# Moving gate tiles of a projection from attention's filling to the stage of the masks

## The chip, the cores and the metric

One core of a Trainium2 chip runs the whole kernel. The metric is device time in microseconds, the median of several runs. Its engines are TensorE (PE, with its weight loads as PEld), VectorE (DVE), ScalarE (ACT), GpSimd (POOL) and SyncE (SP), which issues the loads.

## The reference, cut to what matters

Two layers over 1088 tokens (1024 of a prompt, 64 of a sample) and 1024 features. The change lies in layer 0, where one input projection feeds a sparse attention (a) and a short convolution (b), each with a gate of its own:

```python
q, k, v, ga, qi, ki, wi, gb, gc, xin, gz = _split(h @ w_in, EVEN_SPLITS)
...
top_val, top_idx = lax.top_k(score, topk)
...
logits = jnp.einsum('bqgrd,bqkgd->bqgrk', q, kg).astype(jnp.float32) * (HEAD_DIM ** -0.5)
p = jax.nn.softmax(logits, axis=-1).astype(v.dtype)
...
a_out = o * jax.nn.silu(ga)
...
b_out = gb * y * jax.nn.silu(gz)
out = jnp.concatenate([a_out, b_out], axis=-1) @ w_out
```

Eight heads attend in four pairs; a query's keys are its 256 best by the indexer's score (144 for the sample).

## The kernel before, in words

A projection tile is 128 output features. It takes 72 matmuls: three chunks of tokens (364, 364, 360), eight feature tiles each, and three products each, since weights and activations are split into a high and a low part (`w_hi`, `w_lo`, `ah`, `al`). A weight tile passes through SP (load of `w_raw`), ACT (`w_hi`, L238) and POOL (`w_lo`, L239); there are two places for it, used in turn, so that a tile's `w_hi` can be written only when PE is through with the tile before the last.

Layer 0 goes in stages. The indexer's scores come first, then the search for the threshold of every row (`topk`), beside which PE runs most of the projections. Then DVE makes the masks (`mask`, L592 to L607, seven blocks of rows, tile `bias`). Attention follows (`attend`, L711): for each of the four head pairs t, eight blocks of 128 queries and one block of the sample. For a block PE makes logits (L620), DVE adds the mask and finds the extreme (L622), ACT takes the exponential (L625), POOL scales (L627), PE transposes (L650), ACT and DVE split the result into high and low part (L276 `pth`, L277 `ptl`), and PE multiplies by the values (L658). At a pair's start ACT and POOL prepare its queries (`qst`, L698 and L699).

Eleven projection tiles are left for this time: three of q, four of gate b (`GB`), four of gate a (`GA`), in a fixed order (L47):

```python
ATTN_TILES = [(Q_, 1), (Q_, 2), (Q_, 3), (GB, 0), (GB, 1), (GA, 0), (GB, 2), (GA, 1), (GB, 3), (GA, 2), (GA, 3)]
```

They are a generator, `tiles()` in `layer0` (L919), that issues one matmul (L262) for each call of `next`. Gate a of pair t multiplies the finished output of that pair, so it is held back:

```python
kind, t = left[0]
while kind == GA and self.done <= t:
    yield
```

`BEFORE` calls are made ahead of attention (L932); they come into the program behind the masks, but PE has no other work then and runs them early. `RATE` holds three counts for each pair: calls after each piece of logits (L621), after each pass of `weighted` (L660), and after its transposes (L652). A call that meets a held tile issues nothing. What is left after attention runs behind it. A chunk of gate b is read out of PSUM by DVE (L894, tile `bo`), of gate a by ACT (L909, tile `ga`), which takes the SiLU when the tile is whole (L911); POOL then multiplies (L912). After the last tile ACT and DVE split the mixer's output into `ah` and `al`, and the output projection (`op`, L247) begins. A scheduler decides in what order the instructions stand in each engine's queue.

Of the kernel before, what the change touches and what calls it, by code (L numbers as in the profile page):

```python
# [84 lines left out]
ORDER = [(0, 1, 2, 3, 4, 5, 6, 7)] + [(7, 0, 6, 1, 5, 2, 4, 3)] * 3  # L85


BEFORE = 255
RATE = ((1, 1, 3),) * 4


def cut(n):
# [5 lines left out]
class Trunk:  # L98
# [663 lines left out]
    def layer0(self):  # L762
# [41 lines left out]
        with ExitStack() as es:  # L804
# [74 lines left out]
            with self.pool("attn", "right") as ap:  # L879
# [39 lines left out]
                def tiles():  # L919
                    while left:  # L920
# [3 lines that stand above are left out]
                        key, w = ahead.pop(0)  # L924
                        assert key == (kind, t)
                        fetch()
                        yield from self.steps(w, evacs[kind](t), n=1)
                        left.pop(0)
                        yield

                self.side = tiles()
                for _ in range(BEFORE):  # L932
                    next(self.side)
                for t in range(4):
                    while (Q_, t) in left:
                        next(self.side)
                    self.rate = RATE[t]
                    st = self.pair_stack(ap, t)
# [282 lines left out]
```

## Time and profile before

| | us |
|---|---|
| median of 3 runs (1161.16 to 1162.71) | 1161.26 |
| the profiled execution | 1162.17 |
| its span, first to last instruction | 1160.5 |
| PE busy | 1087.5 (94%) |
| DVE busy | 670.2 (58%) |
| ACT busy | 519.3 (45%) |
| POOL busy | 440.1 (38%) |

The span is what the trace covers; the profiled execution's own time is 1.7 us longer. Busy times are sums over the whole span, and the stages differ: a change in one is read from the rows of that stage, which a later section has.

### The profile page before, as it was taken

What the parts mean: (1) busy time and instruction counts of PE and PEld (TensorE: products, weight loads), DVE (VectorE), ACT (ScalarE), POOL (GpSimd) and SP (SyncE); (2) the same over time, 40 slices, a digit from 0 to 9 for tenths busy, and PEclk for the clock granted to TensorE, in tenths of its full rate; (3) what the DMA queues carried; (4) which work ended last, traced back from release to release, by engine and by line L of the source; (5) the groups of instructions that cost most, each with busy time, mean ns of one, the idle gap of its engine ahead of it and who ended that gap; (6) DMA issues with size and microseconds to landing.
All of it is one profiled execution on the core that took longest, in us unless ns stands there. A gap on an engine that the chain in (4) does not pass through costs nothing.

```text
span 1160.5 us, 18892 instructions
## 1 busy us (share of the span) xinstructions
PE 1087.5 (94%) x7255; PEld 1044.7 (90%) x7255; DVE 670.2 (58%) x1657; ACT 519.3 (45%) x976; POOL 440.1 (38%) x454
## 2 busy tenths in 40 slices
PE   5899999999999449999999899999999999999997
PEld 4789689999999439989899899999999999999996
DVE  4711799998886987767675524521186055247134
ACT  5232586856777246777666313521121211135111
POOL 2634223466548225464431326531143111154222
PEclk9999999999999769999999999999999999999999
DMA  9745511211101000000002410111112111131012
GB/s 361 302 155 191 201 29 55 80 52 38 37 19 54 25 14 19 19 19 20 19 20 82 160 59 31 44 55 37 37 47 91 37 37 36 38 108 38 1 65 91
DMA packets 26074, 81.84 MB, mean 71 GB/s; under 512 B 3072, under 2 KB 9984, under 8 KB 23552
## 3 DMA queue, kind: packets, MB, share of 16 engines
q1 hardware_dynamic: 25984, 80.63, 19.7%
q8 instruction: 57, 0.93, 0.3%
q14 instruction: 33, 0.27, 0.1%
HBM read 74.50 MB, written 6.12 MB: 69 GB/s over the span
## 4 chain that ended last, share of the span: by engine, by line
PE 81%; DVE 7%; ACT 5%; POOL 3%; issue 3%; DMA 1%; SPq 0%; POOLq 0%; DVEq 0%; ACTq 0%
PE pj L247 40%; PE op L247 15%; PE pj L262 9%; PE av L658 3%; PE logit_ps L620 2%; PE p_ps L650 2%; PE ada_ps L153 2%; PE sgu_ps L1036 1%; PE score_ps L427 1%; PE first L318 1%; POOL w_lo L239 1%; POOL hf L329 1%; DVE cum L604 1%; PE score_ps L428 1%; DVE al L277 1%
## 5 line engine op out<-in xcount | busy, mean ns | idle before, releaser
L247 PE MATMUL pj<-ah,w_hi 128*128 128x364 f32 (+1 forms) x984 | 326.0, 331 | 1.0 <-ACT w_hi L238 1.0
L247 PE MATMUL pj<-al,w_hi 128*128 128x364 f32 (+1 forms) x984 | 323.8, 329 | 0.0
L247 PE MATMUL pj<-ah,w_lo 128*128 128x364 f32 (+1 forms) x984 | 323.1, 329 | 0.0
L239 POOL TENSOR_TENSOR w_lo<-w_raw,w_hi 128x1024 fp32r<-128x1024 f32 x63 | 158.0, 2510 | 341.3 <-ACT w_hi L238 336.4
L247 PEld LDWEIGHTS pj<-ah,w_hi 128*128 128x128 f32 x984 | 185.0, 188 | 2.0 <-ACT w_hi L238 1.3
L247 PEld LDWEIGHTS pj<-ah,w_lo 128*128 128x128 f32 x984 | 184.8, 188 | 0.3 <-issue 0.2
L247 PEld LDWEIGHTS pj<-al,w_hi 128*128 128x128 f32 x984 | 185.0, 188 | 0.0
L247 PE MATMUL op<-ah,w_lo 128*128 128x448 f32 (+2 forms) x384 | 126.2, 330 | 3.1 <-POOL w_lo L239 3.1
L247 PE MATMUL op<-al,w_hi 128*128 128x448 f32 (+2 forms) x384 | 126.5, 330 | 0.7 <-DVE al L277 0.6
L247 PE MATMUL op<-ah,w_hi 128*128 128x448 f32 (+2 forms) x384 | 126.9, 330 | 0.0
L238 ACT ACTIVATE w_hi<-w_raw 128x1024 fp32r<-128x1024 f32 x69 | 72.9, 1058 | 111.6 <-PE pj L247 83.2
L528 DVE TENSOR_SCALAR_CACHE_REDUCE cum<-S,cand 128x512 bf16<-128x512 f32 (+5 forms) x142 | 119.0, 838 | 2.0
L262 PE MATMUL pj<-ah,w_hi 128*128 128x364 f32 (+1 forms) x288 | 96.0, 334 | 0.0
L262 PE MATMUL pj<-ah,w_lo 128*128 128x364 f32 (+1 forms) x288 | 95.2, 330 | 0.0
L262 PE MATMUL pj<-al,w_hi 128*128 128x364 f32 (+1 forms) x288 | 95.1, 330 | 0.0
L976 DVE SCALAR_TENSOR_TENSOR x<-op,mod,x 128x192 f32<-128x192 f32 (+2 forms) x64 | 30.5, 497 | 108.2 <-PE op L247 108.2
L555 ACT ACTIVATE junk<-S,cand 128x896 bf16<-128x896 f32 (+2 forms) x78 | 77.7, 996 | 24.4 <-DVE m L558 20.6
L627 POOL TENSOR_SCALAR S<-S,sm 128x384 f32<-128x384 f32 (+8 forms) x68 | 50.8, 753 | 87.1 <-DVE sm L626 72.7
L620 PE MATMUL logit_ps<-kp,qst 128*128 128x384 f32 (+5 forms) x192 | 49.6, 366 | 33.2 <-DVE sm L622 32.6
L247 PEld LDWEIGHTS op<-ah,w_lo 128*128 128x128 f32 x384 | 73.1, 190 | 5.4 <-POOL w_lo L239 3.5
L247 PEld LDWEIGHTS op<-al,w_hi 128*128 128x128 f32 x384 | 73.0, 190 | 3.4 <-DVE al L277 1.4
L247 PEld LDWEIGHTS op<-ah,w_hi 128*128 128x128 f32 x384 | 73.0, 190 | 2.0
(242 smaller groups left out, 1973.9 us busy)
## 6 DMA issues: line engine op xcount, KB each, us to landing
w_raw<-in_w SPq DMA_DIRECT2D x53, 512.0 KB, 3.4
ada<-in_ada_w SPq DMA_DIRECT2D x19, 1024.0 KB, 7.8
w_raw<-in_wo SPq DMA_DIRECT2D x16, 512.0 KB, 3.4
x<-in_x SPq DMA_DIRECT2D x8, 544.0 KB, 6.5
bo<-in_ada_w SPq DMA_DIRECT2D x4, 1024.0 KB, 6.9
x<-in_x SPq DMA_DIRECT2D x1, 1792.0 KB, 10.2
out_y<-x SPq DMA_DIRECT2D x1, 1792.0 KB, 6.6
x<-in_x SPq DMA_DIRECT2D x1, 1536.0 KB, 8.2
```

What stands on the lines that cost most here:

```text
L153: nc.tensor.matmul(pt[32 * g:32 * g + 32, 0:P], self.cs[:, kt, :], raw(kt)[:, g * P:(g + 1) * P], start=kt == 0, stop=kt == KT - 1, tile_p ...
L238: nc.scalar.activation(hi, raw, AF.Copy)
L239: (nc.gpsimd if lo_eng == "pool" else nc.vector).tensor_sub(lo, raw, hi)
L247: last = self.nc.tensor.matmul(ps, wt[:, kt, :], at[:, kt, c0:c1], start=n == 0, stop=n == len(mms) - 1)
L262: self.nc.tensor.matmul(ps, wt[:, kt, :], at[:, kt, a:b], start=kt == 0 and i == 0, stop=kt == KT - 1 and i == 2)
L528: V.tensor_scalar(junks[0][:, 0:SW[j]], self.S[:, span(j)], thr, 0.0, op0=OP.is_lt, op1=OP.add, accum_out=col(cv, j))
L555: nc.scalar.activation(junks[1][:, 0:SW[j]], self.S[:, span(j)], AF.Sign, scale=-1.0, bias=col(cand, j), accum_out=col(cv, j))
L620: mm = nc.tensor.matmul(pt[:, 0:w], lhs, keys[i][:, g, s], start=i == 0, stop=i == 1)
L627: nc.gpsimd.tensor_scalar(p, p, st[:, 3:4], 0.0, op0=OP.mult, op1=OP.add)
L650: mm = nc.tensor.transpose(pt[0:r, o:o + P], p[:, j * P:j * P + r], self.ident)
L658: mm = nc.tensor.matmul(av[:, 0:m], self.vs[0:r, vbase + j, g, :], t[0:r, o:o + m], start=j == 0 and i == 0, stop=j == nj - 1 and i == 1)
L976: nc.vector.scalar_tensor_tensor(x[:, t, a:b], ps[:, a:b], self.mod[l][:, 16 + t, j:j + 1], x[:, t, a:b], op0=OP.mult, op1=OP.add)
```

## The change

Two numbers change. `BEFORE` goes from 255 to 435 calls, and the count after the transposes goes from 3 to 1 for every pair. The order of the tiles stays.

```diff
-BEFORE = 255
-RATE = ((1, 1, 3),) * 4
+BEFORE = 435
+RATE = ((1, 1, 1),) * 4
```

Three places show what this does in the queues. The first is PE at the start of attention, where block 4 of pair 0 (two pieces of 320 keys) gets its logits while the first blocks are transposed. Before:

```order
L650 MATMUL p_ps_4262<-ident_69,S_603 128x128
L262 MATMUL pj_4217<-ah_64,w_lo_4104 128x364
L262 MATMUL pj_4217<-ah_64,w_hi_4103 128x364
L262 MATMUL pj_4217<-al_65,w_hi_4103 128x364
L650 MATMUL p_ps_4298<-ident_69,S_603 128x128
L620 MATMUL logit_ps_4438<-kp0_1903,qst_4233 128x320
L620 MATMUL logit_ps_4438<-kp1_1904,qst_4233 128x320
L650 MATMUL p_ps_4298<-ident_69,S_603 128x128 x3
L262 MATMUL pj_4307<-ah_64,w_hi_4103 128x360
L262 MATMUL pj_4307<-al_65,w_hi_4103 128x360
L620 MATMUL logit_ps_4454<-kp0_1903,qst_4234 128x320
L620 MATMUL logit_ps_4454<-kp1_1904,qst_4234 128x320
```

The same place now:

```order
L620 MATMUL logit_ps_4518<-kp0_1903,qst_4353 128x320
L620 MATMUL logit_ps_4518<-kp1_1904,qst_4353 128x320
L650 MATMUL p_ps_4380<-ident_69,S_603 128x128 x2
L620 MATMUL logit_ps_4522<-kp0_1903,qst_4353 128x320
L650 MATMUL p_ps_4410<-ident_69,S_603 128x128
L620 MATMUL logit_ps_4522<-kp1_1904,qst_4353 128x320
L650 MATMUL p_ps_4410<-ident_69,S_603 128x128 x3
L620 MATMUL logit_ps_4530<-kp0_1903,qst_4354 128x320
L620 MATMUL logit_ps_4530<-kp1_1904,qst_4354 128x320
L620 MATMUL logit_ps_4534<-kp0_1903,qst_4354 128x320
L620 MATMUL logit_ps_4534<-kp1_1904,qst_4354 128x320
```

The filling (L262, `pj`) is gone here, and up to the end of pair 0's sample block hardly any of it is left.

The second place is DVE while it makes the masks:

```order
 L604 SCALAR_TENSOR_TENSOR cum<-ones,cv,bias 128x384
+L894 TENSOR_TENSOR bo<-bo,pj 128x364
 L605 SCALAR_TENSOR_TENSOR bias<-cum,bias 128x384
 L606 SCALAR_TENSOR_TENSOR bias<-S,T,bias 128x384
 L604 SCALAR_TENSOR_TENSOR cum<-ones,cv,bias 128x512
 L607 TENSOR_SCALAR bias<-bias 128x384
+L894 TENSOR_TENSOR bo<-bo,pj 128x360
 L605 SCALAR_TENSOR_TENSOR bias<-cum,bias 128x512
 L606 SCALAR_TENSOR_TENSOR bias<-S,T,bias 128x512
```

Reads of gate b's PSUM now stand between the steps of the masks: these two and three more further on. Before, only one stood there.

The third place is ACT, and behind it POOL, just ahead of attention, where pair 0's queries are prepared. ACT:

```order
 L238 ACTIVATE w_hi<-w_raw 128x1024
 L772 ACTIVATE q<-pj 128x360
+L238 ACTIVATE w_hi<-w_raw 128x1024 x2
 L698 ACTIVATE qst<-q 64x512 x2
 L698 ACTIVATE qst<-q 64x576 x2
```

POOL:

```order
 L760 TENSOR_TENSOR bo<-bo,gc 128x64
 L584 MEMSET cv 128x1 x4
-L239 TENSOR_TENSOR w_lo<-w_raw,w_hi 128x1024 x2
+L239 TENSOR_TENSOR w_lo<-w_raw,w_hi 128x1024 x4
 L699 TENSOR_TENSOR qst<-q,qst 64x512 x2
 L699 TENSOR_TENSOR qst<-q,qst 64x576 x2
```

Two more weight tiles, of gate a 0 and gate b 2, are now split ahead of the queries.

## Rows read from the trace of the kernel before

**Rows 1.** Windows by stage: busy us of each engine (instructions), PEclk, DMA share, GB/s.
```profile
346.80:390.50 43.70, 43.65 (x265) 43.44 (x263) 34.41 (x116) 31.31 (x58) 29.82 (x33) 1.00 0.16 52
390.50:420.00 29.50, 0.00 (x0) 0.00 (x0) 29.19 (x34) 0.14 (x1) 1.95 (x2) 0.56 0.00 0
420.00:478.30 58.30, 54.83 (x349) 50.68 (x349) 43.70 (x149) 42.26 (x96) 30.32 (x35) 0.93 0.06 17
478.30:621.60 143.30, 138.48 (x950) 131.10 (x949) 98.17 (x305) 98.06 (x205) 58.68 (x58) 1.00 0.06 19
621.60:640.10 18.50, 18.42 (x102) 17.25 (x102) 12.96 (x28) 16.04 (x34) 7.07 (x3) 1.00 0.36 128
640.10:643.20 3.10, 0.04 (x1) 0.04 (x1) 2.86 (x4) 1.01 (x2) 3.01 (x1) 0.99 0.00 0
```

**Rows 2.** Chain of waits, in order of time (start, us, what).
```profile
347.01 34.43 PE pj L262 x207
...
476.94 1.45 PE av L658 x10
```

**Rows 3.** Timeline of PE around the masks (start, us, instruction, [idle before, releaser]).
```profile
390.05 0.40 PE L620 MATMUL logit_ps<-kp,qst 128*128 128x256 f32 x2
420.35 0.80 PE L620 MATMUL logit_ps<-kp,qst 128*128 128x256 f32 x2 [29.91 <-DVE sm L622]
```

**Rows 4.** Timeline of DVE in the masks and at their end.
```profile
392.86 0.52 DVE L894 TENSOR_TENSOR bo<-bo,pj 128x364 f32<-128x364 f32 x1
393.31 1.34 DVE L603 TENSOR_SCALAR bias<-S,T 128x896 bf16<-128x896 f32 x2
...
420.01 0.28 DVE L622 CUSTOM_DVE_ANT_0 S<-logit_ps,corner 128x128 f32<-128x128 f32 x1
```

**Rows 5.** Timeline of ACT, then POOL, ahead of attention; last, POOL near 638 us.
```profile
382.86 1.06 ACT L238 ACTIVATE w_hi<-w_raw 128x1024 fp32r<-128x1024 f32 x1 [1.44 <-issue]
...
384.18 2.69 ACT L698 ACTIVATE qst<-q 64x512 fp32r<-64x512 f32 x4
419.86 0.69 ACT L709 ACTIVATE kc<-kp 128x64 fp32r<-128x64 f32 x4 [32.99 <-DVE bias L606]
...
384.00 2.40 POOL L239 TENSOR_TENSOR w_lo<-w_raw,w_hi 128x1024 fp32r<-128x1024 f32 x1 [9.54 <-ACT w_hi L238]
386.48 6.04 POOL L699 TENSOR_TENSOR qst<-q,qst 64x512 fp32r<-64x512 f32 x4
...
637.98 5.13 POOL L239 TENSOR_TENSOR w_lo<-w_raw,w_hi 128x1024 fp32r<-128x1024 f32 x1 [9.08 <-ACT w_hi L238]
```

**Rows 6.** Windows at the start of attention, columns as in rows 1.
```profile
420.00:424.00 4.00, 1.68 (x4) 1.00 (x4) 1.16 (x9) 3.13 (x10) 1.23 (x3) 0.50 0.13 33
...
424.00:437.00 13.00, 12.96 (x75) 12.09 (x75) 11.86 (x49) 10.67 (x28) 7.98 (x13) 0.84 0.08 21
```

**Rows 7.** DVE's groups by line, 420 to 478.3 us: reads of gate b.
```profile
L894 DVE TENSOR_TENSOR bo<-bo,pj 128x364 f32<-128x364 f32 (+1 forms) x5 | 2.6, 526 | 0.8 <-PE pj L262 0.7
```

**Rows 8.** PE's waits, 478.3 to 621.6 us (total us, times, longest).
```profile
PE av L658 <- ACT pth L276: 1.2, 1, 1.2
PE p_ps L650 <- DVE ptl L277: 1.0, 1, 1.0
```

**Rows 9.** ACT's groups by shape in attention: queries, and the SiLU of gate a.
```profile
L698 ACT ACTIVATE qst<-q 64x576 fp32r<-64x576 f32 x6 | 4.0, 668 | 0.0
...
L911 ACT ACT_TABLE_LOAD x2 | 2.6, 1283 | 0.0
L911 ACT ACTIVATE ga<-ga 128x1088 f32<-128x1088 f32 x2 | 2.2, 1112 | 0.0
```

**Rows 10.** Windows of one us where PE's clock falls and rises, columns as in rows 1.
```profile
393.00:394.00 1.00, 0.00 (x0) 0.00 (x0) 1.00 (x3) 0.00 (x0) 0.00 (x0) 0.98 0.00 0
394.00:395.00 1.00, 0.00 (x0) 0.00 (x0) 1.00 (x3) 0.00 (x0) 0.00 (x0) 0.50 0.00 0
427.00:428.00 1.00, 1.00 (x6) 0.96 (x6) 0.97 (x4) 1.00 (x4) 0.62 (x2) 0.50 0.00 0
428.00:429.00 1.00, 1.00 (x9) 0.97 (x8) 0.48 (x4) 0.90 (x3) 1.00 (x2) 0.95 0.00 0
```

## The prediction

> **What bounds the kernel now.** I read the windows by stage first. In the masks PE does nothing for 29.5 us and DVE is busy for 29.19 of them [rows 1]: DVE sets that stage alone. PE stands at a pair of logits that needs DVE, with 29.91 us of idle before it [rows 3]. In attention PE is busy for 54.83 of 58.3 us up to the end of pair 0's sample block (its last multiplication by the values is in [rows 2]) and for 138.48 of 143.3 in the other three pairs, while DVE (43.70 and 98.17) and ACT (42.26 and 98.06) have room [rows 1]: PE is the bound, because the filling fills what the chain of a block leaves open. Then PE is dense until 640.1, and 3.1 us follow in which POOL makes a weight part that PE needs.
>
> One filling matmul costs 0.166 us: 207 of them take 34.43 us on the chain [rows 2].
>
> **What moves.** Counted in PE's queue, the filling is now 255 matmuls ahead of attention, 112 up to the end of pair 0's sample block, 349 in the rest of attention, 76 behind it. With the change it is 360, 5, 246 and 181. The words "three tiles" promise more than happens: of the 180 added calls only 105 issue a matmul (what was left of gate b 0, and gate b 1). The next tile is gate a 0, which is held until pair 0 is done, so 75 calls find nothing, and so do pair 0's own. Pair 0 loses its filling altogether, the others about 34 matmuls each, and 105 more run behind attention. PE's total work is the same; what decides is where it waits.
>
> **The masks.** 105 matmuls at 0.166 are 17.4 us, which lie inside PE's 29.5 idle us. On DVE, which sets this stage, five more reads of gate b come in. One holds DVE up by 0.45 us (392.86 to 393.31) [rows 4], so +2.3 us. Were DVE to wait for PE there it would cost more, but PE ends a chunk each 4 us and has the last one at 389.3 + 17.4 = 406.8, while the read of it stands behind the steps of the block of 896, which DVE reached after 409. I take 2.3; ends 2.3 and 4.
>
> **Pair 0.** Without filling DVE becomes the bound. It is busy for 43.70 us up to the end of the sample block [rows 1]; 2.6 of them are the five reads that move [rows 7], which leaves 41.1. The first 4 us hold 1.2 of it, since exponentials must come first [rows 6]; that start stays. The other 39.9 go at the share that DVE reaches when it is pressed. No row has attention without filling. The nearest is 424 to 437, where the first blocks run with few filling matmuls between them: 11.86 of 13 us, 0.91 [rows 6]. That gives 43.8 + 4 = 47.8 us in place of 58.3: -10.5. PE without its 112 matmuls (18.6 us) needs less than 40. For the ends I take shares of 0.95 (46.0 us, -12.3) and 0.88 (49.3 us, -9.0); the far end is the share in the other pairs, 98.17 of 143.3 or 0.69, at which nothing would be gained.
>
> **Pairs 1 to 3.** 103 matmuls fewer are -17.1 us if every one of them shortens the stretch. PE's waits there are short and come where ACT is held by something else: 1.2 us for `pth`, 1.0 for `ptl` [rows 8]. Such holds are the SiLU of gate a (table load 1.28, 1.11 for the tile, and the table of the exponential again) and the queries (four of 0.65) [rows 9], about 3 us each and two to a pair. In that time the chain moves on by some two passes, and each pass now has about two matmuls of filling instead of four, 0.33 us less cover: two holds of two passes are 1.3 us, say 1.5 a pair, 4.5 in all. So -12.6; ends -17.1 (no new waits) and -8.1 (3 us a pair).
>
> The trace shows PE busy for 0.97 of this stretch and its weight loads for 0.91 [rows 1]. The Trainium skill (Perfetto Trace Analysis, section Identifying the Most-Contended Engine) says that matmul busy time is a poor measure of TensorE's headroom and that the busy share of weight loads is a better one. By it 0.09 of the stretch is already loose and the removed matmuls would shorten it by 0.91 of 17.1 instead: an estimate of 1.5 us less gain, which would leave the sum at -1.9.
>
> **Behind attention.** 105 more matmuls at 0.166: +17.4. PE is busy for 18.42 of the 18.5 us there [rows 1], so nothing hides them. The three added tiles bring their weight splits to engines that have room. The 3.1 us behind it follow the last tile as before and stay.
>
> **The sum.** 2.3 - 10.5 - 12.6 + 17.4 = -3.4 us. The profiled execution took 1162.17, so 1158.8; the median of the runs lies 0.9 below it, so 1157.9 against 1161.26. With the ends of this case (-6.7 to +1.1) that is 1154.6 to 1162.4. A measurement of this kernel can tell about 0.2%, 2.3 us, from no change.
>
> **Rivals.**
>
> *The filling was cover, and waits take its place (slower).* In pair 0 each pass goes from PE's transposes over ACT's and DVE's split back to PE, with two buffers, and ACT has nearly as much to do as DVE (42.26 against 43.70) [rows 1]. If the two wait for each other, DVE's share is 0.80: 49.9 + 4 = 53.9 us, only -4.4; and the other pairs wait 3 us each. 2.3 - 4.4 - 8.1 + 17.4 = +7.2, that is 1168.5. It decides once pair 0 takes over 51.2 us, a DVE share under 0.845, with the other pairs as forecast. For it speaks that the share is 0.69 in the other pairs; against it, that PE and not the chain set their pace, and the 0.91.
>
> *All of it comes out (faster).* If pairs 1 to 3 have no new waits: 2.3 - 10.5 - 17.1 + 17.4 = -7.9, 1153.4. PE's few waits there [rows 8] speak for it; that each came with full filling around it speaks against it.
>
> *The first logits are late.* On ACT, pair 0's queries now stand behind the weights of gate a 0 and gate b 2, and the latter's place is free only when gate b 1 is through, at 406.8; they ran at 384.18 before [rows 5]. An ACT row that waits holds all behind it: `kc` waited 32.99 us and nothing else ran on ACT in them [rows 5]. From 406.8: `w_hi` 1.1, `w_lo` 2.4, two of POOL's four query parts 3.0 [rows 5]: 413.3, and DVE wants the logits at 420.0 + 2.3 = 422.3. Even with POOL at the 5.13 us that a `w_lo` took near 638 [rows 5], a factor of 2.1, it is 406.8 + 1.1 + 5.1 + 6.4 = 419.4. So it costs nothing; if all four parts are needed at the slow pace (425.8), 3.5 us, which makes the whole +0.1 and 1161.4. The Trainium skill (PSUM — Partial Sum Buffer, section Engine vs sequencer instructions) states that the queues of ScalarE, VectorE and GpSimd are strictly first in, first out. By that rule the queries cannot pass the waiting weights, and the trace agrees with its 32.99 us.
>
> *PE's clock stays low longer.* It fell to the 1.2 GHz level at 394 after 3.5 idle us and rose to 2.4 GHz at 428, when PE had been at work again since 423 [rows 10]. With the change it falls later, and pair 0 has nothing dense to raise it. PE's own work of pair 0 is at most 54.83 - 18.6 = 36.2 us in 47.8, so 10 us of it need 7.6 at the high level and 15.1 at the low one: 5.1 us lost for every 10 that it lasts longer, +1.7 in all and 1163.0. Against it: there was little filling before 428 either.
>
> **How the numbers follow.** The forecast 0.47, waits in the filling's place 0.28, all of it out 0.15, late logits 0.05, low clock 0.05. Faster by over 0.2%: some 0.7 of the forecast's range and all of the third, 0.48. Slower: most of the second and a little of the others, 0.26. Within 0.2%: 0.26. The range goes from a little under "all of it out" to the waits' 1168.5: 1152.5 to 1168.5. The likeliest case's own range is 1154.6 to 1162.4.
>
> **What would show it.** Right: PE idle between gate b 1 and the first DVE-bound logits about 13 to 16 us instead of 29.9; `bias` done 2 to 3 us later against the start of the masks; pair 0's stretch near 48 us with DVE over 0.88 busy; the other three near 131 us; 17 us more of dense filling behind attention. Wrong: pair 0 over 51 us with PE waiting for `pth` or `ptl` again and again; DVE waiting at L894 for PE in the masks; logits waiting for `qst`; a low clock beyond 435.

## The result and the profile after

The change makes the kernel slower: 1171.47 us (median of four, 1169.26 to 1173.27) against 1161.21, a ratio of 1.0084 with a 95% interval of 1.0063 to 1.0105. The profiled execution took 1170.45 us with a span of 1168.7, 8.2 more than before. It came to the masks 2.2 us sooner than the execution of before (first L602 at 379.24 against 381.44), in a part that the change does not touch, so the stages have to explain 10.4.

The windows by stage of the changed kernel, cut at the same events as those of every kernel below: the first step of the masks (L602), the first logits that DVE reads (L622), the last multiplication by the values of each pair's sample block (L658), and the first matmul of the output projection. Columns as in rows 1.

```profile
379.20:424.20 45.00, 27.43 (x160) 26.65 (x158) 44.78 (x55) 6.28 (x11) 17.28 (x7) 0.83 0.11 38
424.20:475.20 51.00, 43.70 (x245) 34.91 (x246) 40.51 (x144) 40.00 (x94) 26.91 (x33) 0.90 0.03 9
475.20:520.70 45.50, 43.33 (x276) 38.91 (x275) 34.56 (x109) 30.80 (x69) 17.46 (x20) 0.94 0.00 1
520.70:567.50 46.80, 43.21 (x281) 37.79 (x281) 35.31 (x117) 35.94 (x76) 23.36 (x24) 1.00 0.04 12
567.50:611.90 44.40, 42.88 (x292) 39.77 (x292) 26.31 (x79) 23.15 (x51) 9.07 (x10) 1.00 0.04 13
611.90:642.90 31.00, 30.38 (x182) 30.08 (x182) 8.14 (x17) 15.62 (x28) 12.20 (x5) 1.00 0.32 110
```

The kernel before, cut in the same way: the masks, the three later pairs, and the part behind attention (pair 0 is in [rows 1]).

```profile
381.40:420.00 38.60, 9.05 (x57) 8.84 (x55) 38.25 (x50) 4.10 (x8) 8.22 (x5) 0.66 0.05 17
...
478.40:526.60 48.20, 45.73 (x311) 42.60 (x311) 34.67 (x109) 36.46 (x75) 23.45 (x23) 1.00 0.07 23
526.60:575.50 48.90, 47.72 (x327) 45.13 (x327) 35.84 (x116) 34.53 (x76) 22.42 (x24) 1.00 0.04 12
575.50:621.60 46.10, 44.94 (x313) 43.28 (x313) 27.67 (x80) 26.96 (x55) 12.71 (x13) 1.00 0.07 24
621.60:634.20 12.60, 12.60 (x76) 12.60 (x77) 7.06 (x13) 10.55 (x21) 4.94 (x2) 1.00 0.51 184
```

| stage | before | changed | difference | forecast |
|---|---|---|---|---|
| masks | 38.6 | 45.0 | +6.4 | +2.3 |
| pair 0 | 58.4 | 51.0 | -7.4 | -10.5 |
| pairs 1 to 3 | 143.2 | 136.7 | -6.5 | -12.6 |
| behind attention, up to the output projection | 12.6 | 31.0 | +18.4 | +17.4 |
| from the output projection on | 526.3 | 525.8 | -0.5 | 0 |
| sum | | | +10.4 | -3.4 |

All four signs are as forecast, and the work moved as the queues said: PE issues 160 matmuls in the masks where there were 57, and 182 behind attention where there were 76. What is wrong is the size of three of the four terms.

**In the masks** DVE is busy throughout (44.78 of 45 us) and does not wait for PE at the reads of gate b. But some of its steps take longer. Timeline of DVE, changed kernel:

```profile
385.60 1.80 DVE L603 TENSOR_SCALAR bias<-S,T 128x384 bf16<-128x384 f32 x4
...
394.43 2.77 DVE L606 SCALAR_TENSOR_TENSOR bias<-S,T,bias 128x512 bf16<-128x512 f32 x1
...
406.92 2.43 DVE L607 TENSOR_SCALAR bias<-bias 128x768 bf16<-128x768 bf16 x1
409.27 2.15 DVE L605 SCALAR_TENSOR_TENSOR bias<-cum,bias 128x896 bf16<-128x896 bf16 x1
...
413.42 3.48 DVE L604 TENSOR_TENSOR_SCAN cum<-ones,cv,bias 128x1024 bf16<-128x1024 f32 x1
```

The same steps before:

```profile
387.80 5.14 DVE L603 TENSOR_SCALAR bias<-S,T 128x384 bf16<-128x384 f32 x4
...
399.23 0.75 DVE L606 SCALAR_TENSOR_TENSOR bias<-S,T,bias 128x512 bf16<-128x512 f32 x1
...
409.06 0.33 DVE L607 TENSOR_SCALAR bias<-bias 128x768 bf16<-128x768 bf16 x1
409.31 1.08 DVE L605 SCALAR_TENSOR_TENSOR bias<-cum,bias 128x896 bf16<-128x896 bf16 x1
...
411.50 2.34 DVE L604 TENSOR_TENSOR_SCAN cum<-ones,cv,bias 128x1024 bf16<-128x1024 f32 x1
```

And POOL in the changed kernel:

```profile
393.79 2.86 POOL L239 TENSOR_TENSOR w_lo<-w_raw,w_hi 128x1024 fp32r<-128x1024 f32 x1 [9.57 <-ACT w_hi L238]
405.77 3.36 POOL L239 TENSOR_TENSOR w_lo<-w_raw,w_hi 128x1024 fp32r<-128x1024 f32 x1 [9.13 <-ACT w_hi L238]
409.22 8.88 POOL L699 TENSOR_TENSOR qst<-q,qst 64x512 fp32r<-64x512 f32 x4
```

A DVE step that is long is one that ran beside POOL: L606 at 394.43 beside the first weight split, L607 at 406.92 beside the second, L605 and L604 beside the queries. Before, the queries stood beside L603 (6.04 us from 386.48 [rows 5]), and there L603 took 5.14 us in place of 1.80. So this cost was in the kernel already, 3.3 us of it; the change moved it and made it larger.

**In attention** PE now waits in many small pieces. Waits of PE's weight loads in pairs 1 to 3 of the changed kernel (475.2 to 611.9; total us, times, longest):

```profile
PEld av L658 <- ACT pth L276: 4.2, 7, 1.1
PEld av L658 <- DVE ptl L277: 3.5, 8, 0.5
...
PEld p_ps L650 <- DVE ptl L277: 0.7, 2, 0.4
```

The same waits before (478.4 to 621.6):

```profile
PEld p_ps L650 <- DVE ptl L277: 1.4, 2, 1.3
PEld av L658 <- ACT pth L276: 1.4, 1, 1.4
...
PEld av L658 <- DVE ptl L277: 0.6, 2, 0.3
```

Together they are 8.4 us where they were 3.4. The matmuls' own idle time, of which [rows 8] has the two longest pieces before, grew by less: 7.3 us in place of 4.8, by the windows above.

The clock fell a second time, at the end of pair 0. A line of PE's timeline in the changed kernel, then windows of one us, columns as in rows 1:

```profile
473.21 0.30 PE L658 MATMUL av<-pth,vs 128*128 128x128 f32 x1 [1.40 <-DVE q L722]
```

```profile
472.00:473.00 1.00, 0.00 (x0) 0.00 (x0) 0.67 (x3) 0.69 (x3) 1.00 (x3) 1.00 0.00 0
473.00:474.00 1.00, 0.79 (x7) 0.82 (x7) 0.34 (x2) 0.00 (x0) 0.37 (x1) 0.91 0.00 0
474.00:475.00 1.00, 1.00 (x5) 0.88 (x4) 0.00 (x0) 0.59 (x1) 0.00 (x0) 0.50 0.00 0
...
480.00:481.00 1.00, 1.00 (x7) 0.97 (x7) 0.68 (x2) 0.29 (x1) 0.90 (x1) 0.68 0.00 0
```

PE did nothing in one of them (472): it waited for `q`, and the end of the sample block has next to no filling beside it. From 473.8 to 480.7 it worked at the 1.2 GHz level. That is the start of pair 1, whose clock over the whole pair is 0.94. Before, the clock was at 1.00 in the three later pairs.

### The profile page after: what moved, and what is told of

Same layout as the page of the kernel before. It is cut to its first block, busy times and chain, and to the rows that moved or that the text cites. A ratio compares the mean times of both kernels' runs of the same rounds, so it can differ in the third digit from the quotient of the medians.

```text
span 1168.7 us, 18881 instructions
## 1 busy us (share of the span) xinstructions
PE 1100.6 (94%) x7255; PEld 1047.5 (90%) x7255; DVE 671.9 (57%) x1657; ACT 515.3 (44%) x974; POOL 444.6 (38%) x454
## 4 chain that ended last, share of the span: by engine, by line
PE 78%; DVE 9%; ACT 5%; issue 3%; POOL 2%; DMA 2%; SPq 0%; POOLq 0%; DVEq 0%; ACTq 0%
PE pj L247 40%; PE op L247 15%; PE pj L262 8%; PE av L658 3%; PE logit_ps L620 2%; PE p_ps L650 2%; PE ada_ps L153 1%; PE sgu_ps L1036 1%; PE score_ps L427 1%; PE first L318 1%; POOL w_lo L239 1%; DVE cum L604 1%; POOL hf L329 1%; PE score_ps L428 1%; ACT S L625 1%
## 5 line engine op out<-in xcount | busy, mean ns | idle before, releaser
L239 POOL TENSOR_TENSOR w_lo<-w_raw,w_hi 128x1024 fp32r<-128x1024 f32 x63 | 159.4, 2532 | 378.6 <-ACT w_hi L238 374.8
L262 PE MATMUL pj<-ah,w_hi 128*128 128x364 f32 (+1 forms) x288 | 95.4, 332 | 0.6 <-DVE bo L894 0.6
L262 PE MATMUL pj<-ah,w_lo 128*128 128x364 f32 (+1 forms) x288 | 95.2, 331 | 0.0
L262 PE MATMUL pj<-al,w_hi 128*128 128x364 f32 (+1 forms) x288 | 95.2, 331 | 0.0
L627 POOL TENSOR_SCALAR S<-S,sm 128x256 f32<-128x256 f32 (+8 forms) x68 | 50.7, 751 | 79.5 <-DVE sm L626 69.9
L984 POOL TENSOR_TENSOR acc<-acc,sq 128x448 f32<-128x448 f32 (+2 forms) x40 | 40.0, 1000 | 90.0 <-ACT sq L982 89.3
```

The lines of the kernel that those rows point to most:

```text
L239: (nc.gpsimd if lo_eng == "pool" else nc.vector).tensor_sub(lo, raw, hi)
L262: self.nc.tensor.matmul(ps, wt[:, kt, :], at[:, kt, a:b], start=kt == 0 and i == 0, stop=kt == KT - 1 and i == 2)
L627: nc.gpsimd.tensor_scalar(p, p, st[:, 3:4], 0.0, op0=OP.mult, op1=OP.add)
L984: nc.gpsimd.tensor_add(acc, acc, sq)
```

## The experiments

Theory 1 after the result: filling inside attention is cover, of which only a part of the time returns when it is taken out (13.9 of the 34.9 us that 210 matmuls take at 0.166, 40%), while behind attention the same matmuls cost all of their time; and the masks grew because POOL's work now stands beside the wrong steps of DVE. The rivals: PE bounds attention after all and the loss is in front; or the moved reads of gate b are what costs in the masks.

**One half of the change: the calls ahead of attention alone.**

```diff
 BEFORE = 435
-RATE = ((1, 1, 1),) * 4
+RATE = ((1, 1, 3),) * 4
```

> Only the calls ahead of attention are raised to 435; the filling inside the pairs keeps its old count of three, so pairs 1 to 3 and the part behind attention have as many filling matmuls as before (103, 111, 135 and 76). Theory 1 (filling inside attention is cover for the chain of a block, and taking it out returns only some 41% of its time): masks +6.4 us, pair 0 -7.9 as in the changed kernel, pairs 1 to 3 near 143 us and the tail unchanged, so about 1160 us against 1161.2, and 11 us less than the changed kernel. Rival (the moved reads of gate b and the weight splits ahead of the queries are what costs, wherever the rest of the filling goes): at least +5 us against before, 1166 or more.

Measured: 1159.4 us, ratio 0.9990 (0.9978 to 1.0003), no change that is clear of noise. Its windows of the masks and of pair 0:

```profile
380.00:425.00 45.00, 27.38 (x160) 26.60 (x158) 44.82 (x56) 6.30 (x10) 17.28 (x7) 0.84 0.12 38
425.00:474.30 49.30, 42.38 (x247) 33.67 (x248) 40.35 (x144) 39.74 (x94) 26.86 (x33) 0.94 0.03 9
```

Pairs 1 to 3 take 143.5 us and the part behind attention 12.7. This half of the change gains 9.1 us in pair 0 and loses 6.4 in the masks, and the rest stays. The net loss comes with the other half: from this kernel to the changed one pairs 1 to 3 give back 6.8 us (143.5 to 136.7) and the part behind attention takes 18.3 more. Pair 0 takes 1.7 more too, with 5 filling matmuls in place of 7, which is not explained. The rival falls.

**The other half alone: the count after the transposes.**

```diff
 BEFORE = 255
-RATE = ((1, 1, 3),) * 4
+RATE = ((1, 1, 1),) * 4
```

> Only the count after the transposes goes from three to one; the calls ahead of attention stay 255, so masks and queries stay as before. The filling is 255, 70, 67, 71, 78 and 251: 175 matmuls (29.1 us at 0.166) leave attention and run behind it. Theory 1 (41% of their time returns in attention): attention some 12 us shorter, the tail 29 us longer, about +17, 1178 us. Rival (PE bounds attention, all of the time returns): 0, 1161 us. Rival (filling is free, none returns): +29, 1190 us.

Measured: 1171.9 us, ratio 1.0102 (1.0088 to 1.0115). Slower, but by 11 us and not by 17: a miss for the size. Windows of pairs 1 to 3 and of the part behind attention in this kernel:

```profile
471.50:515.00 43.50, 40.95 (x277) 37.20 (x277) 34.97 (x111) 31.45 (x69) 19.88 (x21) 1.00 0.04 13
515.00:561.10 46.10, 42.67 (x284) 38.06 (x283) 33.69 (x115) 36.16 (x77) 23.06 (x24) 1.00 0.04 12
561.10:601.60 40.50, 37.84 (x259) 34.20 (x258) 26.83 (x79) 22.86 (x51) 9.28 (x11) 1.00 0.04 14
601.60:643.40 41.80, 41.80 (x252) 41.80 (x252) 8.71 (x18) 16.03 (x29) 12.22 (x5) 1.00 0.24 82
```

Behind attention the 175 matmuls cost 29.2 us (41.8 against 12.6), which is 0.167 each: there nothing hides them. In attention 17.8 us return, 61%, and unevenly: pair 1 loses 36 matmuls (6.0 us) and 4.7 us of its time, pair 2 40 (6.6) and 2.8, pair 3 57 (9.5) and 5.6, pair 0 42 (7.0) and 4.7. So a single share for all of attention was too simple. Pair 0 keeps 70 filling matmuls here, and the clock stays at 1.00 in the pairs behind it. Pair 1 is the plainest: 43.5 us here with 67 filling matmuls, 45.5 in the changed kernel with 65. And it is pair 2 that returns least. The SiLU of gate a 0 lies in it now; before, one lay in pair 1 and one at the seam of pairs 2 and 3, as ACT's timeline of the kernel before shows:

```profile
511.36 1.11 ACT L911 ACTIVATE ga<-ga 128x1088 f32<-128x1088 f32 x1
...
576.09 1.11 ACT L911 ACTIVATE ga<-ga 128x1088 f32<-128x1088 f32 x1
```

So pairs 1 to 3 have one SiLU where they had two, pair 1 none and pair 2 one, in this kernel as in the changed one. The next experiments look at these two pairs.

**The order of the tiles, so that three tiles really move.**

```diff
-... (GB, 1), (GA, 0), (GB, 2), (GA, 1), (GB, 3), (GA, 2) ...
+... (GB, 1), (GB, 2), (GA, 0), (GB, 3), (GA, 1), (GA, 2) ...
```

> The changed kernel with gate b 2 ahead of gate a 0 and gate b 3 ahead of gate a 1, so that the 180 added calls nearly all issue a matmul; the filling is 432, 5, 65, 67, 93 and 130: 72 more matmuls in the masks, 51 fewer behind attention, 21 fewer in the last pair. Theory 1: masks +3 us against the changed kernel, attention -1.4 (41% of 3.5), tail -8.5, together -7, about 1164.5. Rival (the masks are the harm: each read moved there costs 1.3 us as the first five did): masks +8, so about -2, 1169.

Measured: 1161.2 us, ratio 1.0011 (1.0000 to 1.0021), 10 us better than the changed kernel, more than either expectation. Against it: masks +2.0, pair 0 -1.3, pairs 1 to 3 -3.4, behind attention -6.1. (This profiled execution was the slowest of its twelve, 1165.16, with 3 us more in the rest of the program, so the stages are compared and not the sums.) Three more reads of gate b and 72 matmuls cost the masks only 2.0 us, so the rival falls. Behind attention 51 matmuls fewer gave 6.1 us and not the expected 8.5: PE stands idle there for 2.7 of 24.9 us. And pair 1, with the same 65 filling matmuls as in the changed kernel, has the full clock:

```profile
476.60:520.30 43.70, 41.14 (x276) 36.78 (x275) 34.37 (x109) 31.07 (x70) 17.47 (x20) 1.00 0.00 1
```

43.7 us at 1.00 against 45.5 at 0.94. The price of the low clock at the start of pair 1 is thus some 1.8 us. It is a comparison of two kernels that differ elsewhere too; a kernel that changes the clock alone was not tried. But the other runs lie in the same order: with this filling pair 1 takes 44.9 us at 0.96 (the late splits, below), and with 103 matmuls 48.2 at 1.00 (before) against 49.5 at 0.97 (the first experiment). In this kernel the clock falls in pair 2 instead, which takes 48.0 us at 0.96 where the changed kernel takes 46.8 at 1.00.

**The SiLU of gate a 0 left out.** Its place is taken by a plain copy of the same shape, so this kernel computes no SiLU for that gate tile.

```diff
-nc.scalar.activation(g, g, AF.Silu)
+nc.scalar.activation(g, g, AF.Copy if t == 0 else AF.Silu)
```

> The changed kernel with the SiLU of gate a 0 left out (a plain copy of the same shape in its place), so that ACT loads no table for it and none for the exponentials behind it: two loads of 1.28 us less in pair 2, where the filling is 67 matmuls. Theory 1a (with thin filling a hold of ACT goes straight through to PE): pair 2 falls from 46.8 us by 2 to 3. Rival (what keeps pair 2 long is the loop of split, transposes and multiplications itself, at every pass): by less than 0.5.

Timeline of ACT in the changed kernel, pair 2:

```profile
524.45 1.28 ACT L911 ACT_TABLE_LOAD   x1
525.74 1.11 ACT L911 ACTIVATE ga<-ga 128x1088 f32<-128x1088 f32 x1
...
527.36 1.28 ACT L625 ACT_TABLE_LOAD   x1
```

With the copy the two table loads are gone, and the window of pair 2 reads:

```profile
521.00:565.40 44.40, 42.55 (x282) 37.91 (x282) 35.19 (x117) 33.28 (x75) 23.28 (x24) 1.00 0.04 13
```

Measured: pair 2 takes 44.4 us in place of 46.8, and the other five stages stay within 0.1. (The whole took 1170.37 us, because what lies outside these stages took 2.6 us more in this one execution.) That is -2.4, for two loads of 1.28 (2.56) on an engine that is busy for 36 of 47 us. In this pair, with 67 filling matmuls, a hold of ACT goes almost whole to PE. The same step was not tried with full filling, but its holds were not free there: the two waits of [rows 8] end at 513.63 and 578.47, each little more than 1 us behind the end of one of the two SiLUs before.

**The weight splits moved away from the masks.** The changed kernel, with the splits of gate a 0 and gate b 2 issued behind the exponential and the scaling of pair 0's eighth block:

```diff
...
-key, w = ahead.pop(0)
...
-fetch()
+late = (kind, t) == (GA, 0)
+with ExitStack() as behind:
+    if late:
+        for mark in self.marks[7]:
+            behind.enter_context(self.tc.issue_after(mark))
+        fetch()
+    key, w = ahead.pop(0)
...
+    if key != (GB, 1):
+        fetch()
```

`marks` holds the exponential and the scaling of each block; its lines are left out here.

> The changed kernel, but the weight splits of gate a 0 and gate b 2 are issued behind pair 0's eighth block, so pair 0's queries are made early again and POOL is not at work beside the later masks; the filling counts are those of the changed kernel. Theory 1 with contention (DVE's mask steps are stretched while POOL works beside them): the mask stage falls from 45.0 to about 41 us, so about -4 against the changed kernel, 1167. Rival (the mask stage grew through the moved reads of gate b, not through POOL's place): no difference, 1171.

Measured: 1165.72 us, ratio 1.0051 (1.0038 to 1.0064), 5.8 us better than the changed kernel: 4.3 in the masks, 0.9 in pair 0, 0.6 in pair 1. The masks' window:

```profile
379.90:420.60 40.70, 27.95 (x160) 27.45 (x158) 40.16 (x55) 4.05 (x8) 8.22 (x5) 0.87 0.05 17
```

The masks take 40.7 us: +2.1 against before, with all five added reads of gate b in them. The reads cost what the prediction said (+2.3); the other 4.3 us were POOL's. The queries are early again, and L603 beside them takes 5.15 us (from 386.27), as before.

**More of POOL's work beside the masks, and nothing else.** The kernel before, with one weight split's subtraction done three times:

```diff
-(nc.gpsimd if lo_eng == "pool" else nc.vector).tensor_sub(lo, raw, hi)
+for _ in range(self.again):
+    (nc.gpsimd if lo_eng == "pool" else nc.vector).tensor_sub(lo, raw, hi)
...
+self.again = 3 if key == (GB, 1) else 1
```

> The kernel before, with POOL's subtraction for the low weight part of gate b 1 (2.4 us, beside the masks) done three times instead of once; nothing else moves, and POOL has nothing due there until the queries. Contention theory (DVE's mask steps are stretched while POOL works beside them, some 2 us for each subtraction of 2.4 to 2.9): the stage of the masks grows from 38.6 us by 3 to 4. Rival (the stage grows only by the reads of gate b that move into it): 38.6 us as before, total 1161.

Measured, one execution: 1166.25 us against 1160.77 for before on the same chip, with a span 4.0 longer than the one shown of before. POOL's and DVE's timelines of this kernel (lines are shifted by two, L605 is L603 of the other kernels):

```profile
384.21 7.30 POOL L241 TENSOR_TENSOR w_lo<-w_raw,w_hi 128x1024 fp32r<-128x1024 f32 x3 [9.54 <-ACT w_hi L239]
391.58 6.22 POOL L701 TENSOR_TENSOR qst<-q,qst 64x512 fp32r<-64x512 f32 x4
```

```profile
387.99 6.81 DVE L605 TENSOR_SCALAR bias<-S,T 128x384 bf16<-128x384 f32 x4
...
395.17 3.62 DVE L605 TENSOR_SCALAR bias<-S,T 128x896 bf16<-128x896 f32 x3
```

L603's two groups take 6.81 and 3.62 us where they took 5.14 and 1.77, together 3.5 more, and the masks end 42.1 us after they began in place of 38.6. The added work, for whose result nobody waits, made DVE later by 3.5 us.

The Trainium skill (SBUF — State Buffer, section SBUF: two separate sides) has a rule for this: VectorE and GpSimd share one pair of SBUF ports, a VectorE operation in a 2-port mode, or with two SBUF inputs beside a GpSimd operation that reads SBUF, and the GpSimd operation exclude each other, and whichever comes second waits for the whole instruction of the first. The traces here agree: L606 at 394.43 ends at 397.20, 0.55 us after the split beside it (393.79 + 2.86 = 396.65), and takes 0.75 us alone. POOL pays too, 2.86 and 3.36 us in place of 2.40; the longer one started at 405.77 beside L604, which was already at work (404.93) and took 2.07 us as before (2.08).

**Two versions from these prices.** First the late splits with the full count in the pairs:

```diff
 BEFORE = 435
-RATE = ((1, 1, 1),) * 4
+RATE = ((1, 1, 3),) * 4
```

> The first experiment's settings (435 calls ahead, three calls after the transposes) together with the late weight splits: filling 360, 7, 103, 111, 135 and 76. If the two effects are separate and add up: masks 40.7 us (+2.1 against before), pair 0 near 49.5 (-8.9), pairs 1 to 3 and the tail as before, so about -6 against before, 1155 us. If the late splits only shift POOL's work onto pair 0 or pair 1, which now are needed in full: 1159 as in the first experiment.

Measured: 1155.46 us, ratio 0.9950 (0.9938 to 0.9962). The windows of the masks and of pair 0 (pairs 1 to 3 take 143.2 us, the part behind attention 12.7):

```profile
381.70:422.40 40.70, 27.93 (x160) 27.43 (x158) 40.14 (x55) 4.04 (x8) 8.22 (x5) 0.87 0.05 17
422.40:472.50 50.10, 42.80 (x247) 33.69 (x247) 40.24 (x144) 41.59 (x96) 31.33 (x35) 0.94 0.10 30
```

+2.1 - 8.3 + 0 + 0.1 = -6.1, as the two effects add up to, and 1155 was expected. Then the same with gate b 2 ahead of gate a 0:

```diff
-... (GB, 1), (GA, 0), (GB, 2), (GA, 1), (GB, 3), (GA, 2) ...
+... (GB, 1), (GB, 2), (GA, 0), (GB, 3), (GA, 1), (GA, 2) ...
...
-if key != (GB, 1):
+if key != (GB, 2):
```

> As the run before it, with gate b 2 ahead of gate a 0, so that 432 matmuls run ahead of attention, and the splits of gate a 0 and gate b 3 late: filling 432, 7, 103, 113, 137 and none behind the last multiplication by the values. By the prices measured so far: masks about 44 us (+5.4), pair 0 49.5 (-8.9), pairs 1 to 3 with some 2 more matmuls than before (143), of which the last 72 in pair 3 take the place of the 76 behind attention (-12 if the end of attention can follow at once, 0 if the output projection then waits as long for the last block): between 1152 and 1160, 1156 as the likeliest.

Measured: 1154.47 us, ratio 0.9951 (0.9938 to 0.9964), the same as the run before it within the interval. The masks take 44.0 us, as expected, and pair 0 51.4, 1.9 more than expected. The 72 matmuls that no longer stand behind attention are not a gain by themselves. Stretches in PE's timeline of this kernel:

```profile
612.73 0.43 PE L262 MATMUL pj<-ah,w_hi 128*128 128x360 f32 x1 [1.78 <-ACT ga L907]
...
625.86 0.36 PE L659 MATMUL av<-pth,vs 128*128 128x256 f32 x1 [2.64 <-DVE q L723]
```

PE's last multiplications by the values now end at 631.1, and in the 20 us before that PE stands idle three times (1.78 and 2.64 us here, and 1.07 at 629.62). DVE and ACT have the last blocks and the split for the output projection to do at once: by this reading the 76 matmuls behind attention were cover as well, for the end of the last pair. No run tests that by itself. Both versions are some 0.5% faster than the kernel before, and faster than the changed one.

## Why the prediction was wrong

**Forecast 1157.9 (1152.5 to 1168.5), measured 1171.47.** The terms of the sum were the right ones; three had the wrong size, all to the slow side: +4.1 in the masks, +3.1 in pair 0, +6.1 in pairs 1 to 3, +1.0 behind attention, -0.5 in the rest, 13.8 together (from -3.4 to +10.4). The range of the likeliest case was too narrow as well: the ends that the terms name add up to -9.7 and +4.3, where the sum has -6.7 and +1.1. The result lies outside both.

**The masks, forecast +2.3, measured +6.4.** "On DVE, which sets this stage, five more reads of gate b come in" was right: 2.1 us of it, as the run with late splits shows. The step that failed is the sentence that the late queries cost nothing. It asked only whether they would be ready when DVE wants the logits, and they were (L699 ended at 418.10, the logits were read at 424.22). It did not ask what two more weight splits and the queries do to DVE while they run. The trace of before told it: L239 took 5.13 us near 638 and 2.40 at 384 [rows 5], and two pieces of L603, the first of 896 columns, took 1.34 us [rows 4] where four, beside the queries, took 5.14. The factor of 2.1 was used as a slow pace for POOL and not read as two engines in each other's way.

**Pair 0, forecast 47.8, measured 51.0** (49.3 to 51.4 in the six other runs with next to no filling in it). The step that failed is the DVE share of 0.91, taken from 13 us of the start for everything behind the first 4 us. Measured there it is 38.95 of 47.0 us, 0.83. The same 13 us do have 0.90 without filling, the two stretches of 13 us behind them 0.86 and 0.88; it is the end of the pair, with the sample block, that falls off. The first and the last of these stretches in the changed kernel:

```profile
428.20:441.20 13.00, 12.75 (x64) 10.25 (x63) 11.74 (x50) 10.78 (x29) 8.45 (x14) 0.82 0.06 20
...
467.20:475.20 8.00, 6.59 (x41) 5.21 (x40) 4.59 (x17) 5.48 (x13) 3.15 (x5) 0.91 0.00 0
```

At 0.91 these 4.59 us of DVE would have taken 5.0 and not 8.0. In the last 8 us PE waits 1.40 us for DVE's `q`, and then DVE 2.38 us for PE's transposes (until 475.75). Whether filling would close this gap was not tested by itself. The measured share lies between the forecast's and the rival's 0.80, and under its deciding 0.845; the 51.2 us that went with 0.845 were not passed, because DVE had 1.0 us less to do than was forecast.

**Pairs 1 to 3, forecast -12.6, measured -6.5.** The step that failed is "1.5 a pair, 4.5 in all" for new waits. Of the 17.1 us taken out, 10.6 did not return. Some 1.8 of them are the low clock at the start of pair 1, and the waits of the weight loads for `pth` and `ptl`, most of a few tenths of a us, grew by 5.0. The other 4 or so are not accounted for. The holds of ACT that the prediction priced explain little of it, as far as is known: one SiLU costs 2.4 us here, but before there were two in these pairs, with 1.19 and 1.04 us of PE's idle time behind them. The prediction thought the rest of the chain hidden. That PE's few waits before [rows 8] were few because of the filling is what the first two experiments bear out: with the filling back, pairs 1 to 3 take 143.5 us, and without it more small waits stand there.

**The low clock** was a rival, priced at 5.1 us for every 10 us that it lasts longer in pair 0. There it lasted hardly longer: PE was back at the 2.4 GHz level at 432.8, 8.6 us behind DVE's first logits, where it was 8.0 before (428.0 [rows 10]). It came in another place: at the seam of pairs 0 and 1, behind 1.40 us in which PE had nothing to do.

**Behind attention, forecast +17.4, measured +18.4.** Right, and the second experiment gives it again: 0.167 us for each matmul.

The rival "the filling was cover, and waits take its place" named the mechanism, and its 1168.5 lies 3 us under the result. It had the masks at +2.3; with the +6.4 that they took it would have given 1172.6. That it comes so near is in part luck: pair 0 gained 3.0 us more than it says (-7.4 for -4.4), and pairs 1 to 3 1.6 less (-6.5 for -8.1).

## What to carry to other kernels

An engine that is busy for 0.97 of a stretch because filler sits in its gaps is not bound by the filler: taking filler out returned 40 to 60% of its time here, and 175 of these matmuls put behind the stage cost all of their time. Before moving work, ask where it will stand as the only work, and where as cover. And an engine that nobody waits for can still make another one late: look at which instructions run side by side in the new order, and whether the trace already has the same instruction at two durations.

## What the runs showed of the hardware

- DVE's steps of the masks stretch beside POOL's subtractions (0.75 to 2.77, 0.33 to 2.43, 1.08 to 2.15, 2.34 to 3.48 us), and POOL's beside DVE's (2.40 to 3.36 for a weight split, 6.04 to 8.88 for the queries). L602, which also writes an accumulator, does not: for 128x576 it took 0.87 us before, beside the queries (387.01), and 0.87 in the changed kernel, with nothing on POOL (384.81).
- PE's granted clock fell from the 2.4 to the 1.2 GHz level at 473.8, behind 1.40 us in which PE waited for `q` (L722), and was back at 480.7, while PE was busy for nearly all of the time between.
- A table load took 1.28 us on ACT, and leaving two of them out made pair 2 of the changed kernel 2.4 us shorter, in one execution.
